# Two decoder layers on one core: order of TensorE work in the attention and delta-rule branches

## The chip, the cores and the metric

The kernel runs on one core of a Trainium2 chip. The metric is the device time of one execution, in microseconds; a kernel's time is the median of its runs. The core has five engines, each with its own instruction queue that is worked through in order: PE (TensorE, matrix products, with its weight loads shown apart as PEld), DVE (VectorE), ACT (ScalarE), POOL (GpSimd) and SP (SyncE, which here only issues DMAs). ACT can issue DMAs too, from the same queue that holds its arithmetic.

## The reference

Two layers, each on 512 tokens of width 1024:

```
xn   = rmsnorm(x)
proj = xn @ w_in                 # columns for all branches and three gate blocks
A    = SSD: causal conv, chunked scan, SiLU-gated rmsnorm
B    = latent attention: q = rmsnorm(cq) @ w_uq  (8 heads, 128 plain + 64 rotated columns each)
       k_nope, v = rmsnorm(ckv) @ w_ukv ; one rotated key shared by the heads ; causal softmax
C    = gated delta rule, chunks of 64:
       (I + a_mat) sol = rhs     # triangular solve in each chunk and head
       v_new = u - w state ; o = q state + qk v_new ; state = state*decay + k^T v_new
h    = x + (sum over branches of sigmoid(gate) * (branch @ w_branch)) @ w_out
x    = h + relu(rmsnorm(h) @ w_up)^2 @ w_down
```

A final rmsnorm follows the second layer. All inputs and outputs are float32.

## The kernel before

**Dense products.** Each float32 operand is split into a high part and a low rest (`hi`, `lo`), and one product is made of three matmuls: hi·hi, hi·lo and lo·hi. The helper `mm3` (lines 178 to 182) issues these three; in this document one call is a *triple*, and its third matmul is line 182. `dense_F` gives a result with features on the partitions, `dense_T` one with tokens there. `weights` (line 162) loads a block of a weight matrix from SP into one of two raw buffers (`wraw`) and splits it with an ACT copy (line 158) and a DVE subtraction (line 159) into one of four pairs `whi`/`wlo`. Results go to four PSUM banks named `acc`; the small products of the branches share three banks named `sm` and one named `yt`.

**Order.** The program is written branch by branch, but a planner that works with estimated costs orders each engine's queue when the program is built: of the instructions whose inputs it takes to be ready, it issues the one written first. The order is then fixed, and what is late on the chip is waited for. An extra dependency without a semaphore (`add_manual_dep` with `NoSync`) tells the planner that one instruction must come after another of the same engine; nothing is waited for at run time because of it.

**Latent attention (head pairs from line 636).** For each of four head pairs: the queries' projection (`q_weights`, 12 triples in three banks: two heads' plain parts and one bank with both rotated parts), the rotation of the queries (`rope`, line 603: four DMAs that swap halves, then three DVE operations; line 676: two more DMAs that swap the heads), the keys' projection (4 triples), the values' projection (8 triples in four banks, line 692), and then for each head scores (lines 703 to 708), softmax, transposes (line 725) and the product with the values (lines 741 to 743). The DMAs of lines 607 and 676 are issued by ACT. Each values' bank is 128x256 and is moved out in two pieces of 128 columns, each with an ACT copy (line 251) and a DVE subtraction (line 252).

**Delta rule.** `gdn_matrix` and `gdn_blocks` build the chunk matrices and invert their 32x32 blocks on DVE; `gdn_inverses` (line 941) joins the blocks into 64x64 inverses with products of 32x32 (lines 956, 966, 968) and 64x64 (lines 977, 981), between which ACT and DVE copy results from PSUM. Meanwhile dense triples of the SSD branch run. `gdn_unit` (line 984) runs twice, for four heads each: after its own projections it walks over four chunks of 128 tokens, and in each come `keys` (line 1036), the solve (line 1042), the state's update (1056), the output's products (1065, 1070). At the end of a unit four groups of transposes (line 1096) turn its result for the output projection.

**Output projections.** `out_proj` goes over four column blocks: first the gate's projection and a tanh, then the branch's projection, which is multiplied with the gate and added to `mixed`.

Order of writing in a layer, counted in triples from the start of attention: attention 0 to 95, keys of the delta rule 96 to 127, SSD group 0 to 207, (inverses), two blocks of attention's output to 271, SSD group 1 to 351, attention's and SSD's outputs to 543, delta-rule unit 0 to 623, unit 1 to 703, delta-rule output 704 to 831. In the first layer 64 triples precede attention (32 each of the two latent projections).

Of the kernel before, what the change touches and what calls it, by code (L numbers as in the profile page):

```python
# [20 lines left out]
P = 128  # L21
S = 512
# [37 lines left out]
def hybrid_kernel(ctx, tc, a, out, depth=2, taps=None):  # L60
# [91 lines left out]

    def split_half(raw, hold=None):

        n = raw.shape[1]
        hi, lo = hold or (mk(wp, [P, n], F32R, "whi"), mk(wp, [P, n], F32R, "wlo"))
        with tc.high_priority():
            act.copy(hi, raw)  # L158
            dve.tensor_tensor(lo, raw, f32(hi), ALU.subtract)  # L159
        return hi, lo  # L160
# [16 lines left out]

    def mm3(o, ah, al, bh, bl, start, stop, more=False):

        pe.matmul(o, ah, bh, start=start, stop=False, skip_group_check=more)  # L180
        pe.matmul(o, ah, bl, start=False, stop=False, skip_group_check=more)  # L181
        pe.matmul(o, al, bh, start=False, stop=stop, skip_group_check=more)  # L182
# [239 lines left out]
    for ly in range(depth):  # L422
# [119 lines left out]
        def seg_exp(pl, o, t, h0):  # L542
# [4 lines left out]
            pe.matmul(ps, w, cum[1][:, t].rearrange("p i l -> p (i l)"), start=True, stop=True)  # L547
# [5 lines left out]

        def out_proj(w2d, br, yh, yl, pl, part=range(4)):
            for dp in part:
                tg = []
                for ps in dense_F(weights(w_in, O_GATE + br * D + dp * 256, 256, D), tiles(256), D, xh, xl):
                    t_ = mk(pl, [P, S], F32, "cva", 2)
                    act.activation(t_, ps, AF.Tanh, scale=0.5)
                    tg.append(t_)  # L560
                for j, ps in enumerate(dense_F(weights(w2d, dp * 256, 256, D), tiles(256), D, yh, yl)):
                    d = 2 * dp + j
                    if mixed[d] is None:
                        mixed[d] = mk(lp, [P, S], F32, "mix", 8)
                        dve.scalar_tensor_tensor(mixed[d], tg[j], 1.0, ps, ALU.add, ALU.mult)
                    else:
                        dve.scalar_tensor_tensor(tg[j], tg[j], 1.0, ps, ALU.add, ALU.mult)
                        dve.tensor_tensor(mixed[d], mixed[d], tg[j], ALU.add)


# [32 lines left out]
        def rope(src):  # L603

            sw_ = mk(lp, [P, S], F32, "mix", 8)
            for i in range(4):
                act.dma_start(sw_[32 * i : 32 * i + 32], src[32 * (i ^ 1) : 32 * (i ^ 1) + 32])
# [26 lines left out]
        scale = (128 + 64) ** -0.5  # L634
        yh, yl = hilo_tags(lp, "y")
        for hp in range(4):
            def q_weights():
                for k0 in (0, 2):
                    raw = mk(wp, [P, 768], F32, "wraw", 2)
                    sync.dma_start(raw.rearrange("p (k n) -> p k n", k=2),  # L640
                                   a["mla_w_uq"][ly][k0 * P : (k0 + 2) * P, hp * 384 : (hp + 1) * 384].rearrange("(k p) n -> p k n", p=P))
                    for k in range(2):
                        rv = raw[:, k * 384 : (k + 1) * 384].rearrange("p (h n) -> p h n", h=2)
                        hi = mk(wp, [P, 384], F32R, "whi")
                        lo = mk(wp, [P, 384], F32R, "wlo")
                        nv = lambda x: x[:, :256].rearrange("p (h n) -> p h n", h=2)
                        pv = lambda x: x[:, 256:].rearrange("p (h n) -> p h n", h=2)
                        act.copy(nv(hi), rv[:, :, :P])
                        act.copy(pv(hi), rv[:, :, P:])
                        dve.tensor_tensor(nv(lo), rv[:, :, :P], f32(nv(hi)), ALU.subtract)  # L650
                        dve.tensor_tensor(pv(lo), rv[:, :, P:], f32(pv(hi)), ALU.subtract)
                        yield k0 + k, hi.unsqueeze(1), lo.unsqueeze(1)

            *pq, pp = dense_F(q_weights(), tiles(384), 512, cqh, cql)

# [13 lines left out]
            qs = head_tiles(pq, "q", scale)  # L669
# [5 lines left out]
            for i in range(2):  # L675
                act.dma_start(qd[64 * i : 64 * i + 64], qr[64 * (1 - i) : 64 * (1 - i) + 64])
            qps = [mk(ml, [P, S], F32R, f"qps{j}") for j in range(2)]
            for j in range(2):
                half, other = (slice(64 * i, 64 * i + 64) for i in (j, 1 - j))
                act.copy(qps[j][half], qr[half])  # L680
                dve.tensor_tensor(qpl[j][half], qr[half], f32(qps[j][half]), ALU.subtract)
                act.copy(qps[j][other], qd[other])
# [5 lines left out]
            def ev(t, ps):  # L688
                for j in range(2):
                    split_act(*(x[:, t, :] for x in vs[j]), ps[:, j * P : (j + 1) * P])  # L690

            dense_T(wkv, 256, 256, ckh, ckl, ev, lambda w: w.rearrange("p (h n) -> p h n", h=2)[:, :, P:])

            for j in range(2):
# [3 lines left out]
                for t in range(T):  # L698
# [4 lines left out]
                    pe.matmul(o, qh[:, tok], kh[:, :n], start=True, stop=False)  # L703
                    pe.matmul(o, qh[:, tok], kl[:, :n], start=False, stop=False)
                    pe.matmul(o, ql[:, tok], kh[:, :n], start=False, stop=False)
                    pe.matmul(o, qps[j][:, tok], kps[:, :n], start=False, stop=False)  # L706
# [13 lines left out]
                for kbs in ((0,), (1,), (3, 2)):  # L720
                    ps = sm_bank()
                    n = 0
                    for kb in kbs:
                        for t in range(kb, T):
                            pe.transpose(ps[:, n : n + P], pn[t][:, kb * P : (kb + 1) * P], ident)  # L725
# [11 lines left out]
                    for kb, c0, c in parts:  # L737
                        v_h, v_l = (x[:, kb, :] for x in vs[j])
                        o = po[:, c0:]
                        w = S - c0  # L740
                        pe.matmul(o, v_h, th[:, c : c + w], start=kb == 0, stop=False)  # L741
# [30 lines left out]
        def ssd_group(g, yh, yl):  # L772
# [14 lines left out]
            for t in range(T):  # L787
                pe.transpose(ps[:, t * P : (t + 1) * P], bt[:, t * P : (t + 1) * P], ident)
            act.activation(btok.rearrange("p t n -> p (t n)"), ps, AF.Copy, scale=0.25)
            for cp in range(2):  # L790
                for j, pj in enumerate(dense_F(weights(w_in, O_XBC + 512 * g + 256 * cp, 256, D), tiles(256), D, xh, xl)):
# [3 lines left out]
                    for t in range(T):  # L795
                        pe.transpose(ps[:, t * P : (t + 1) * P], xf[:, t * P : (t + 1) * P], ident)
# [5 lines left out]
            for t in range(T):  # L802
# [13 lines left out]
                for h in range(8):  # L816
                    pe.matmul(py[:, h * 64 : (h + 1) * 64], e2[h // 4][:, h % 4, :], xd[:, h * 64 : (h + 1) * 64], start=True, stop=True)  # L817
# [28 lines left out]
            for c in range(4):  # L846
                k = 4 * g + c
                ps = y_bank()
                for t in range(T):
                    pe.transpose(ps[:, t * P : (t + 1) * P], z[:, t, c * P : (c + 1) * P], ident)  # L850
# [90 lines left out]
        def gdn_inverses(nts, xs):  # L941
# [9 lines left out]
            for u in range(2):  # L951
                ps = sm_bank()
                q = mk(br, [P, 512], F32, "eE", 2)
                for ev_, od in zip(EV, OD):
                    for i in range(16):
                        pe.matmul(ps[od, i * 32 : (i + 1) * 32], N[u][ev_, i, od], xs[u][ev_, i, :32], start=True, stop=True)
                act.copy(q[OD[0]], ps[OD[0]])
                dve.tensor_copy(q[OD[1]], ps[OD[1]])
                qs.append(q)
            for u in range(2):  # L960
                ps = sm_bank()
                q = qs[u]
                for p_, (ev_, od) in enumerate(zip(EV, OD)):
                    for i in range(16):
                        c = slice(i * 32, (i + 1) * 32)
                        pe.matmul(ps[ev_, c], q[od, c], N[u][od, i, od], start=True, stop=True)
                        if p_ == 0:
                            pe.matmul(ps[od, c], N[u][od, i, od], q[od, c], start=True, stop=True)
                dve.tensor_copy(xs[u][OD[0], :, :32], v32(ps[OD[0]]))
                for ev_, od in zip(EV, OD):  # L970
                    act.copy(N[u][ev_, :, od], v32(ps[ev_]))
            for u in range(2):
                for i0 in (0, 8):
                    ps = sm_bank()
                    q = mk(br, [P, 512], F32, "eE", 2)
                    for i in range(8):
                        pe.matmul(ps[64:, i * 64 : (i + 1) * 64], N[u][:64, i0 + i, 64:], xs[u][:64, i0 + i, :], start=True, stop=True)
                    (dve.tensor_copy if i0 else act.copy)(q[64:], ps[64:])
# [425 lines left out]
```

## Time and profile before

| | |
|---|---|
| runs | 2360.38, 2364.24, 2359.33 us; median 2360.38 |
| the profiled execution | 2360.41 us, its span 2358.6 us |
| PE, share of the span | 99% (PEld 81%) |
| DVE, ACT, POOL | 68%, 48%, 3% |
| mean granted TensorE clock | 0.995 |
| DMA, mean | 94 GB/s |

The span runs from the first to the last instruction; 1.8 us lie around it. A row of groups reads: line, engine, operation, out<-in, shapes, count, then busy time and the mean of one instruction, then the engine's idle time just before them and what ended it. A row of waits reads: who waited, for whom, total, number, longest. A window's row reads: from:to, length, busy time and count of instructions by engine, granted clock, DMA. The durations of matmuls are modelled to the end of their pipeline, so two that follow each other overlap in the profile.

### The profile page before, as it was taken

How to read it: one execution, taken by the hardware profiler on the slowest of the kernel's cores; microseconds unless marked ns; L12 is line 12 of the kernel's file. 1: busy time of each engine (PE TensorE's matmuls, PEld its weight loads, DVE VectorE, ACT ScalarE, POOL GpSimd, SP SyncE). 2: the span in 40 equal slices, each digit the busy share in tenths (PEclk: the TensorE clock that was granted, in tenths of full speed). 3: DMA queues.
4: the chain of work that ended last, by engine and by line, in shares of the span. 5: the costliest groups of instructions: out<-in, count | busy, mean ns of one | idle time of the engine just before them, and what ended most of it. 6: DMA issues, size and time to landing. Idle time of an engine off the chain costs nothing.

```text
span 2358.6 us, 32004 instructions
## 1 busy us (share of the span) xinstructions
PE 2323.6 (99%) x11901; PEld 1911.4 (81%) x11902; DVE 1595.8 (68%) x3183; ACT 1131.9 (48%) x2267; POOL 61.6 (3%) x76
## 2 busy tenths in 40 slices
PE   9999999999999999999999999999999999999998
PEld 7878778888887888888887877888888878888886
DVE  7878865635675468767767789665356655677668
ACT  6655524423343345545656555344234434455545
POOL 1000000000000000000000000000000100000000
PEclk9999999999999999999999999999999999999999
DMA  4222432233222443233132223322333224332231
GB/s 136 85 68 81 117 88 81 81 90 96 84 77 76 137 150 107 71 126 116 40 106 72 72 84 104 97 81 81 98 90 85 76 81 157 129 108 89 90 125 45
DMA packets 196509, 222.77 MB, mean 94 GB/s; under 512 B 31105, under 2 KB 152449, under 8 KB 196353
## 3 DMA queue, kind: packets, MB, share of 16 engines
q1 hardware_dynamic: 193008, 215.92, 30.0%
q10 hardware_dynamic: 3344, 4.80, 0.8%
q8 instruction: 94, 1.54, 0.3%
q14 instruction: 63, 0.51, 0.1%
HBM read 204.44 MB, written 11.53 MB: 92 GB/s over the span
## 4 chain that ended last, share of the span: by engine, by line
PE 92%; DVE 4%; DMA 1%; ACT 1%; POOL 1%; issue 1%; SPq 0%; ACTq 0%; POOLq 0%; DVEq 0%
PE acc L180 23%; PE acc L181 23%; PE acc L182 23%; PE sm L181 2%; PE sm L180 2%; PE sm L182 2%; PE sm L817 1%; PE sm L725 1%; PE sm L1042 1%; PE sm L1065 1%; DVE wlo L159 1%; PE yt L741 1%; DMA mix<-mix 1%; PE sm L1056 1%; PE sm L706 0%
## 5 line engine op out<-in xcount | busy, mean ns | idle before, releaser
L159 DVE TENSOR_TENSOR wlo<-wraw,whi 128x512 fp32r<-128x512 f32 (+1 forms) x552 | 376.8, 685 | 428.0 <-ACT whi L158 421.8
L158 ACT CAST whi<-wraw 128x512 fp32r<-128x512 f32 (+1 forms) x552 | 339.7, 618 | 651.9 <-PE acc L181 456.6
L180 PE MATMUL acc<-xh,whi 128*128 128x512 f32 (+1 forms) x1184 | 458.9, 389 | 2.5 <-DVE vl L252 2.5
L182 PE MATMUL acc<-xh,wlo 128*128 128x512 f32 (+1 forms) x1184 | 459.9, 389 | 0.0
L181 PE MATMUL acc<-xl,whi 128*128 128x512 f32 (+1 forms) x1184 | 458.9, 388 | 0.0
L180 PEld LDWEIGHTS acc<-xh,whi 128*128 128x128 f32 x1184 | 222.9, 189 | 45.7 <-issue 1.8
L182 PEld LDWEIGHTS acc<-xh,wlo 128*128 128x128 f32 x1184 | 223.2, 189 | 43.8 <-issue 0.7
L181 PEld LDWEIGHTS acc<-xl,whi 128*128 128x128 f32 x1184 | 223.3, 189 | 43.5 <-issue 0.5
L182 PE MATMUL acc<-yh,wlo 128*128 128x512 f32 x384 | 151.9, 396 | 0.0
L181 PE MATMUL acc<-yl,whi 128*128 128x512 f32 x384 | 151.2, 394 | 0.0
L180 PE MATMUL acc<-yh,whi 128*128 128x512 f32 x384 | 151.2, 397 | 0.0
L158 ACT CAST whi<-wr 128x512 fp32r<-128x512 f32 x160 | 99.6, 622 | 104.8 <-DVE wlo L159 37.5
L182 PE MATMUL acc<-whi,xl 128*128 128x512 f32 (+1 forms) x352 | 134.3, 384 | 0.0
L180 PE MATMUL acc<-whi,xh 128*128 128x512 f32 (+1 forms) x352 | 134.0, 382 | 0.0
L181 PE MATMUL acc<-wlo,xh 128*128 128x512 f32 (+1 forms) x352 | 133.7, 380 | 0.0
L761 DVE SCALAR_TENSOR_TENSOR cva<-acc,pc,cva 128x511 f32<-128x511 f32 (+2 forms) x168 | 119.7, 743 | 15.0 <-ACT cva L759 8.3
L159 DVE TENSOR_TENSOR wlo<-wr,whi 128x512 fp32r<-128x512 f32 x160 | 109.9, 688 | 28.6 <-ACT whi L158 28.4
L182 PE MATMUL acc<-whi,yl 128*128 128x512 f32 (+1 forms) x260 | 100.4, 386 | 0.0
L180 PE MATMUL acc<-whi,yh 128*128 128x512 f32 (+1 forms) x260 | 100.4, 386 | 0.0
L181 PE MATMUL acc<-wlo,yh 128*128 128x512 f32 (+1 forms) x260 | 100.3, 386 | 0.0
L180 PEld LDWEIGHTS acc<-yh,whi 128*128 128x128 f32 x384 | 71.6, 188 | 16.9 <-ACT yh L255 2.3
L181 PEld LDWEIGHTS acc<-yl,whi 128*128 128x128 f32 x384 | 72.2, 188 | 15.4 <-issue 1.0
(406 smaller groups left out, 4542.5 us busy)
## 6 DMA issues: line engine op xcount, KB each, us to landing
wraw<-in_w_in_dram SPq DMA_DIRECT2D x140, 512.0 KB, 3.7
wraw<-in_w_up_dram SPq DMA_DIRECT2D x64, 512.0 KB, 3.7
wr<-in_w_down_dram SPq DMA_DIRECT2D x32, 1024.0 KB, 5.1
wraw<-in_w_mla_out_dram SPq DMA_DIRECT2D x16, 512.0 KB, 3.5
wraw<-in_w_ssd_out_dram SPq DMA_DIRECT2D x16, 512.0 KB, 3.4
wraw<-in_w_gdn_out_dram SPq DMA_DIRECT2D x16, 512.0 KB, 3.4
wraw<-in_w_out_dram SPq DMA_DIRECT2D x16, 512.0 KB, 3.7
wraw<-in_mla_w_uq_dram SPq DMA_DIRECT2D x16, 384.0 KB, 3.3
```

The costliest lines, as they stand in the source:

```text
L158: act.copy(hi, raw)
L159: dve.tensor_tensor(lo, raw, f32(hi), ALU.subtract)
L180: pe.matmul(o, ah, bh, start=start, stop=False, skip_group_check=more)
L181: pe.matmul(o, ah, bl, start=False, stop=False, skip_group_check=more)
L182: pe.matmul(o, al, bh, start=False, stop=stop, skip_group_check=more)
L725: pe.transpose(ps[:, n : n + P], pn[t][:, kb * P : (kb + 1) * P], ident)
L741: pe.matmul(o, v_h, th[:, c : c + w], start=kb == 0, stop=False)
L761: dve.scalar_tensor_tensor(acc[:, d:], ps[:, : S - d], taps_[3 - d], acc[:, d:], ALU.mult, ALU.add)
L817: pe.matmul(py[:, h * 64 : (h + 1) * 64], e2[h // 4][:, h % 4, :], xd[:, h * 64 : (h + 1) * 64], start=True, stop=True)
L1042: m = pe.matmul(pw[:, h * P : (h + 1) * P], Y[:, h, :], r[:, h * P : (h + 1) * P], start=True, stop=True)
L1056: pe.matmul(pS[:, i * 256 : (i + 1) * 256], ktok[i][:, t, :], vd[:, i * 256 : (i + 1) * 256], start=True, stop=True)
L1065: pe.matmul(po[:, h * P : (h + 1) * P], pt_[:, h, :], vn[:, h * P : (h + 1) * P], start=True, stop=True)
```

## The change

Five edits. (1) The small products and some copies of the delta rule get a key when they are written (`step`), and at the end of a layer `hold_steps` adds a dependency without a semaphore from each one whose key is in the table `BEHIND` to the dense triple of that number (for ACT and DVE: to the last weight split before it). Keys that begin with 0 and a text hold in the first layer only. (2) In attention the queries' rotated part is projected first, in one bank and from weights laid out for it (`uq_r`, `uq_n` are host-side rearrangements of the same matrix), then rotated; the plain parts come after. (3) The values go to two banks of 128x512, each moved out with one copy and one subtraction. (4) The swaps of the rotation go to SP's queue, where the weight loads are. (5) The delta rule's output projection computes the gates of block 0 and 1 before the first branch projection, and stays one block ahead.

```diff
+    BEHIND = {
+        ("solve", 0, 1): 634, ("solve", 0, 3): 669, ("attend", 0, 3): 671, ("solve", 1, 1): 714,
+        ("solve", 1, 2): 723, ("solve", 1, 3): 739, ("out", 0, 0): 687, ("out", 0, 1): 691, ("out", 1, 0): 756,
+        (0, "pair", 1): 311, (0, "left", 0): 314, (0, "right", 0): 317, (0, "left", 1): 319, (0, "right", 1): 322,
+        (0, "paired", 1): 315,
+    }
+    def hold_steps(ly, n):
+        for key, ins in steps:
+            keys = [k[:i] for k in ((ly,) + key, key) for i in range(len(k), 0, -1)]
+            at = next((n + BEHIND[k] for k in keys if k in BEHIND), None)
+            if at is not None:
+                on = triples[at] if ins.engine == pe.engine else next(x[ins.engine] for i, x in reversed(splits) if i <= at)
+                tc.add_manual_dep(ins, on, ... NoSync ...)
...
+        def out_proj_ahead(w2d, br, yh, yl, pl):
+            for dp in (0, 1, None, 2, None, 3, None, None):   # a number: gates; None: the next projection
...
         def rope(src):
-                act.dma_start(sw_[32 * i : 32 * i + 32], src[32 * (i ^ 1) : 32 * (i ^ 1) + 32])
+                sync.dma_start(sw_[32 * i : 32 * i + 32], src[32 * (i ^ 1) : 32 * (i ^ 1) + 32])
...
-            *pq, pp = dense_F(q_weights(), tiles(384), 512, cqh, cql)
-            qs = head_tiles(pq, "q", scale)
+            raw = mk(wp, [P, 512], F32, "wraw", 2)
+            sync.dma_start(raw, a["uq_r"][ly][hp])
+            wh, wl = split_half(raw)
+            pp = acc_bank()
+            for k in range(4):
+                mm3(pp, wh[:, kc], wl[:, kc], cqh[k], cql[k], k == 0, k == 3)
             qp = mk(ml, [P, S], F32, "qp")
             act.mul(qp, pp, scale)
             qr = rope(qp)
-                act.dma_start(qd[64 * i : 64 * i + 64], qr[64 * (1 - i) : 64 * (1 - i) + 64])
+                sync.dma_start(qd[64 * i : 64 * i + 64], qr[64 * (1 - i) : 64 * (1 - i) + 64])
...
+            qs = head_tiles(dense_F(weights(a["uq_n"][ly], hp * 256, 256, 512), tiles(256), 512, cqh, cql), "q", scale)
...
-            vs = [[mk(ml, [P, T, P], F32R, nm, 2) for nm in ("vh", "vl")] for _ in range(2)]
-            dense_T(wkv, 256, 256, ckh, ckl, ev, lambda w: ...)
+            vs = [mk(ml, [P, T, 256], F32R, nm, 1) for nm in ("vh", "vl")]
+            for q in range(2):
+                ps = acc_bank()
+                for t in (2 * q, 2 * q + 1):
+                    o = ps[:, t % 2 * 256 : t % 2 * 256 + 256]
+                    ... mm3(o, ckh[k0 + k][:, tok], ckl[k0 + k][:, tok], vw(wh[:, k, :]), vw(wl[:, k, :]), ...)
+                split_act(*(x[:, 2 * q : 2 * q + 2].rearrange("p t n -> p (t n)") for x in vs), ps)
...
-        out_proj(a["w_gdn_out"][ly], 2, *yg, br)
+        out_proj_ahead(a["w_gdn_out"][ly], 2, *yg, br)
+        hold_steps(ly, n_mla)
```

More of the change, by code (lines that the diff above doesn't have):

```diff
@@ L150, in rope_tables @@
         act.activation(cosT, nn, AF.Sin)
+    triples = []
+    splits = []
     def split_half(raw, hold=None):
@@ L157, in split_half @@
         with tc.high_priority():
-            act.copy(hi, raw)
-            dve.tensor_tensor(lo, raw, f32(hi), ALU.subtract)
+            pair = act.copy(hi, raw), dve.tensor_tensor(lo, raw, f32(hi), ALU.subtract)
+        splits.append((len(triples), {i.ins.engine: i.ins.name for i in pair}))
         return hi, lo
@@ L181, in mm3 @@
         pe.matmul(o, ah, bl, start=False, stop=False, skip_group_check=more)
-        pe.matmul(o, al, bh, start=False, stop=stop, skip_group_check=more)
+        triples.append(pe.matmul(o, al, bh, start=False, stop=stop, skip_group_check=more).ins.name)
     def dense_F(gen, cols, K, xh, xl, mid=None, banks=None):
@@ L552, in hybrid_kernel, with gates, project @@
         mixed = [None] * KD
+        def gates(br, dp, tg):
+            for t_, ps in zip(tg, dense_F(weights(w_in, O_GATE + br * D + dp * 256, 256, D), tiles(256), D, xh, xl)):
+                act.activation(t_, ps, AF.Tanh, scale=0.5)
+            return tg
+        def project(w2d, yh, yl, dp, tg):
+            for j, ps in enumerate(dense_F(weights(w2d, dp * 256, 256, D), tiles(256), D, yh, yl)):
+                d = 2 * dp + j
+                if mixed[d] is None:
+                    mixed[d] = mk(lp, [P, S], F32, "mix", 8)
+                    dve.scalar_tensor_tensor(mixed[d], tg[j], 1.0, ps, ALU.add, ALU.mult)
+                else:
+                    dve.scalar_tensor_tensor(tg[j], tg[j], 1.0, ps, ALU.add, ALU.mult)
+                    dve.tensor_tensor(mixed[d], mixed[d], tg[j], ALU.add)
@@ L554, in out_proj, with pair_tiles @@
+        def pair_tiles(pl):
+            return [mk(pl, [P, S], F32, "cva", 2) for _ in range(2)]
         def out_proj(w2d, br, yh, yl, pl, part=range(4)):
             for dp in part:
[L556 to L568, printed above, removed]
+                project(w2d, yh, yl, dp, gates(br, dp, pair_tiles(pl)))
@@ new lines, in out_proj_ahead @@
+        def out_proj_ahead(w2d, br, yh, yl, pl):
+            tg = {}
+            for dp in (0, 1, None, 2, None, 3, None, None):
+                if dp is None:
+                    d = min(tg)
+                    project(w2d, yh, yl, d, tg.pop(d))
+                    continue
+                if dp % 2:
+                    both = mk(pl, [P, 2, S], F32, "bA" if dp == 1 else "bB")
+                    tg[dp] = gates(br, dp, [both[:, j] for j in range(2)])
+                else:
+                    tg[dp] = gates(br, dp, pair_tiles(pl))
@@ L634, in hybrid_kernel @@
         scale = (128 + 64) ** -0.5
+        n_mla = len(triples)
         yh, yl = hilo_tags(lp, "y")
         for hp in range(4):
[L637 to L652, printed above, removed]
-            *pq, pp = dense_F(q_weights(), tiles(384), 512, cqh, cql)
             def head_tiles(pss, nm, c=None):
@@ L1035, in gdn_unit @@
                     for i in range(2):
-                        pe.matmul(pk[:, i * 256 : (i + 1) * 256], kT[i][:, tok], st[:, i * 256 : (i + 1) * 256], start=True, stop=True)
+                        step(pe.matmul(pk[:, i * 256 : (i + 1) * 256], kT[i][:, tok], st[:, i * 256 : (i + 1) * 256], start=True, stop=True), "keys", u, t)
                     for h in range(4):
@@ L1370, in hybrid_kernel @@
     h_pool.close()
[L1373 removed]
+_INS = ['x', 'positions', 'w_in', 'mla_w_ukv', 'w_ssd_out', 'w_mla_out', 'w_gdn_out', 'w_out', 'w_up',
         'w_down', 'final_norm_g']
```

75 lines of the change are left out of this document (43 added, 32 removed).

## The prediction

> **What bounds the kernel now.** I read the page's busy shares first, then its chain, then the list of who waited for whom on PE, then the granted clock by stretch, and last the queues of ACT and SP in attention.
>
> ```profile
> PE 2323.6 (99%) x11901; PEld 1911.4 (81%) x11902; DVE 1595.8 (68%) x3183; ACT 1131.9 (48%) x2267; POOL 61.6 (3%) x76
> PE 92%; DVE 4%; DMA 1%; ACT 1%; POOL 1%; issue 1%; SPq 0%; ACTq 0%; POOLq 0%; DVEq 0%
> ```
>
> PE sets the time: 99% busy and 92% of the chain. The change takes away no matmul, so it can gain only where PE waits or runs slowly. The waits:
>
> ```profile
> engine line waited for: us in total, times, longest us
> PE acc L180 <- DVE vl L252: 6.2, 5, 1.7
> PE sm L1042 <- DVE tok L1038: 3.1, 6, 0.6
> PE yt L1096 <- DVE tok L1091: 3.0, 4, 0.9
> PE sm L547 <- DVE sg L545: 2.5, 3, 1.2
> ...
> PE sm L706 <- ACT qps L682: 1.3, 2, 0.7
> ...
> PE sm L981 <- DVE eE L978: 0.9, 1, 0.9
> ...
> PE sm L981 <- ACT eE L978: 0.7, 1, 0.7
> PE sm L966 <- ACT eE L957: 0.7, 1, 0.7
> ```
>
> Five lines are what the edits aim at: the values' eviction (vl), the delta rule's solves (L1042) and output transposes (L1096), the rotated part (L706), the inverses (L981, L966). A wait costs a little more than its idle time, because a matmul's shown end lies behind the point at which its successor may start:
>
> ```profile
> 104.23 0.39 PE L182 MATMUL acc<-cqh,wlo 128*128 128x512 f32 x1
> 104.45 0.39 PE L180 MATMUL acc<-cqh,whi 128*128 128x512 f32 x1
> ```
>
> Each lasts 0.39 us and the next starts after 0.23 (a triple is 0.68 us), so I add 0.16 us a wait. (The Trainium skill, "Trainium Kernel Development and Optimization", Performance Expectations, says that matmul busy time is a bad metric because matmuls are pipelined; the 0.39 against 0.23 agrees.) The clock:
>
> ```profile
> 330.42:387.57 57.15, 54.87 (x592) 0.88 0.26 71
> 1506.58:1556.80 50.22, 50.16 (x594) 1.00 0.27 72
> 351.12:364.78 13.66, 12.71 (x102) 10.73 (x101) 3.87 (x6) 5.07 (x9) 0.00 (x0) 0.50 0.26 79
> 1245.41:1248.83 3.42, 3.36 (x8) 2.71 (x9) 2.89 (x9) 0.93 (x5) 0.00 (x0) 0.50 0.59 183
> ```
>
> The first two rows (PE alone) are the same work, the delta rule's inverses with SSD triples around them, in the first and the second layer: 592 and 594 matmuls, 57.15 and 50.22 us. The first layer loses 6.9 us, to the three waits of L966 and L981 and to a stretch of 13.7 us at half clock; the second has neither. The last row is half clock for 3.4 us just behind the second layer's longest vl wait.
>
> **The change part by part.**
>
> *Values in two banks.* Before, four banks are finished together at the end of the values' product and leave in eight pieces:
>
> ```profile
> L251 ACT CAST vh<-acc 128x128 fp32r<-128x128 f32 x64 | 14.3, 277 | 4.7 <-PE acc L182 2.6 <-DVE vl L252 1.5 <-issue 0.2
> L252 DVE TENSOR_TENSOR vl<-acc,vh 128x128 fp32r<-128x128 f32 x64 | 15.2, 282 | 0.0
> L158 ACT CAST whi<-wraw 128x512 fp32r<-128x512 f32 x536 | 332.3, 622 | 640.0 <-PE acc L181 456.6 <-PE acc L182 88.6 <-PE yt L181 25.3
> L159 DVE TENSOR_TENSOR wlo<-wraw,whi 128x512 fp32r<-128x512 f32 x536 | 368.7, 690 | 415.4 <-ACT whi L158 409.3 <-ACT cva L757 1.8 <-PE acc L182 1.5
> ```
>
> Eight pieces are 8 x 0.28 = 2.2 us on each of ACT and DVE; two pieces of 512 columns, by the same operations on 512 columns (L158, L159), 1.2 and 1.4. The first bank now ends half way through the product, and the next dense product needs one bank (the rotated part) where it needed three, while two of four were never taken by values. I let all five waits go: 6.2 + 5 x 0.16 = **7.0 us**, and with them the 3.4 us at half clock, half of it, **1.7 us**. Cover: the keys' two banks must be out before the values end; if not, one eviction, 0.62 + 0.69 = 1.3 us, is paid at each of eight head pairs.
>
> *Rotated part first, swaps on SP.* The order of ACT's queue before one of the vl waits (its end at 130.88):
>
> ```profile
> 126.61 0.55 ACT L251 CAST vh<-acc 128x128 fp32r<-128x128 f32 x2
> 126.90 0.55 ACTq L607 DMA_DIRECT2D mix<-qp  x1
> 127.05 0.41 ACT L648 CAST whi<-wraw 128x256 fp32r<-128x256 f32 x1
> 127.48 1.25 ACTq L607 DMA_DIRECT2D mix<-qp  x2
> 129.22 0.59 ACT L251 CAST yh<-yt 128x512 fp32r<-128x512 f32 x1 [1.76 <-PE yt L743]
> 129.23 0.51 ACTq L607 DMA_DIRECT2D mix<-qp  x1
> 129.78 0.77 ACT L251 CAST vh<-acc 128x128 fp32r<-128x128 f32 x4
> 74.69 0.37 SPq L171 DMA_DIRECT2D wraw<-in_mla_w_ukv_dram  x1
> ```
>
> Four DMA issues stand between the second and the third vh copy, about 0.55 us each. With the two of L676 a head pair spends 6 x 0.55 = 3.3 us of ACT on issues; on SP one takes 0.37 (last row), 2.2 us, and SP has nothing else to do but load. The rotation, which needs two DMAs in a row, now starts 8 triples (5.5 us) earlier against its scores. L706's two waits go: 1.3 + 2 x 0.16 = **1.6 us**. The queries' weights also become three splits of 512 columns in place of eight smaller ones. None of this ACT and DVE time is on the chain by itself; I give it no term.
>
> What SP's move could cost: SP is in order, and its loads wait long.
>
> ```profile
> SPq L171 <- DVE wlo L651: 36.0, 3, 15.4
> 133.01 4.50 DMA mix<-mix
> 1279.04 4.29 DMA mix<-mix
> wraw<-in_mla_w_ukv_dram SPq DMA_DIRECT2D x8, 512.0 KB, 3.6
> ```
>
> A load waits up to 15.4 us for its raw buffer, and a swap queued behind it would wait as well; a load behind a swap waits for the rotation. Loads have time to spare (3.6 us to land against waits of 9 to 15 us for a place), so I take 0; the upper end is one slow swap (4.5 us, the longest rows of the chain) on the path at each of eight head pairs, 36 us, which is the slower rival below. The Trainium skill, "DMA: Bandwidth & Descriptors", Issuing engines are not separate DMA queues, says that issuing from several engines saves only the sequencer's time; by it the move is free, while the same page, Queues, rings and completion order, has each issuing engine own a ring that is drained in order, so that a swap would stand behind a 512 KB load: 3.6 us more for each of two steps. No row here shows swaps on SP's ring.
>
> *Held products.* The numbers in the table against where the products stand now (windows of line 182 alone, the third matmul of a triple; 64 precede the count in the first layer):
>
> ```profile
> 0.00:626.15 626.15, 268.59 (x697) 131.34 (x697) 0.99 0.32 92
> 0.00:661.50 661.50, 282.71 (x732) 137.91 (x732) 0.99 0.32 91
> 0.00:706.00 706.00, 300.90 (x777) 146.30 (x777) 0.99 0.31 90
> 0.00:729.50 729.50, 308.02 (x794) 149.56 (x794) 0.99 0.31 89
> 0.00:737.50 737.50, 310.45 (x800) 150.68 (x800) 0.99 0.31 89
> 0.00:347.25 347.25, 135.30 (x360) 67.63 (x360) 1.00 0.34 98
> ```
>
> The solves that wait stand behind 633, 668 and 713 triples and are held behind 635, 670 and 715 (a number n in the table means n + 1 issued): two triples, 1.36 us, against waits of 0.6 at most and their 0.16. All six go: 3.1 + 6 x 0.16 = **4.1 us**. The chain of chunks behind them moves by the same 1.4 us; the planner moves what follows with it. The output transposes of unit 1 wait at 717 and 737; they are now held behind the triple 756 of 832, where the later one stood behind 736, and the gates computed ahead are the dense work that fills the distance: 3.0 + 4 x 0.16 = **3.6 us**. If the cover were short, they would wait as now. In the last solve's place there is a longer delay (730 to 740 triples, 6.8 us); what waits for it are the transposes alone, 17 triples further on, against 8.0 us from solve to transpose now (729.5 to 737.5). The inverses of the first layer: `pair` stands behind 296 triples with no triple up to 357 us, and is held behind 312, then 2 to 5 triples between each step. If that makes the first layer like the second: **6.9 us**.
>
> *Sum.* 7.0 + 1.7 + 1.6 + 4.1 + 3.6 + 6.9 = 24.9 us. Against it stands that the queue orders are planned anew and that the planner's errors, which made these waits, stay. Lower bound of new waits: none. Upper: every head pair and every held place waits again as long as now, (6.2 + 1.3)/7 + 0.16 = 1.2 us at eight head pairs and 7.7 us in the delta rule, 17.3 us. I take 5, nearer to none, since each removed wait had a cause of its own that is gone. 24.9 - 5 = 19.9. The profiled execution took 2360.41 us, as the median (2360.38): **2340.5 us**.
>
> **The rivals.**
>
> A: the holds only move the waits (the solve's chain through DVE is what is late, and two triples less of cover are missing one chunk on). For it: six waits of almost equal size, one in three chunks. Against: other chunks don't wait. Attention alone: 7.0 + 1.7 + 1.6 = 10.3, time **2350**.
>
> B: the first layer's clock doesn't come back. For it: half clock began at 351.1 behind waits of 0.7 us, so the small products themselves may be too little activity. Against: the second layer runs them at full clock. Of the 6.9 us the waits are 0.9 + 0.7 + 0.7 + 3 x 0.16 = 2.8; 4.1 stay, and perhaps the 1.7: **2345**. The Trainium skill, "TensorE: Matmul & The Clock Gate", HAM oscillation, puts re-throttling to idle gaps over about 3.4 us; by it waits of 0.7 us would not matter. The rows disagree, as no gap here is that long and the clock fell.
>
> C: slower. SP's order puts a swap behind a load that waits for its raw buffer. Place: L706 of each head pair; price: what the swap is late beyond the cover. It decides from 24.9 / 8 = 3.1 us a head pair; at 4.5 us the sum is -24.9 + 36 = +11: **2371**. For it the 15.4 us row; against it that qp is now ready early, and that a raw buffer is freed by splits that PE's own pace sets.
>
> D: no change: new waits (17.3 and more) eat the gain; within 0.2% of before, **2358**.
>
> **How the numbers follow.** Forecast 0.55, A 0.12, B 0.14, C 0.10, D 0.09. About 0.2% (4.7 us) is what this kernel's runs can tell. A, B and the forecast are faster: 0.81, less 0.01 for A's edge; same 0.09; slower 0.10. Range: below, all 24.9 us and the L547 waits (2.5 + 0.5) by a lucky order, 2332; I go to 2330. Above, 24.9 - 17.3 = 7.6 gives 2353, and D's edge takes it to 2357. Forecast's own range 2333 to 2349.
>
> **What would show it.** Right: no row of PE waiting for vl, at most one for L1038 and L1091, the first layer's stretch of inverses at clock 1.00 and about 50 us, no half clock in attention, L607 and L676 on SP. Wrong: rows of L706 waiting for qps or a DMA (C), L1042 still waiting (A), a stretch at 0.50 near the held inverses (B). The whole is wrong if PE's waits shrink and the span doesn't.

## The result

The changed kernel takes **2335.47 us** (median of 4 runs, 2334.5 to 2340.46) against 2361.04 for the kernel before (4 runs beside it, 2359.33 to 2364.24): ratio 0.9896, 95% interval 0.9881 to 0.9911. That is 25.6 us less. The forecast was 2340.5, its range 2330 to 2357. The profiled execution took 2336.03 us (span 2334.1, mean clock 0.998).

The busy shares and the shares of the chain, from the changed kernel's page:

```profile
PE 2314.3 (99%) x11902; PEld 1908.0 (82%) x11902; DVE 1590.1 (68%) x3095; ACT 1123.9 (48%) x2179; POOL 60.1 (3%) x76
PE 95%; DVE 2%; ACT 1%; DMA 1%; POOL 0%; issue 0%; SPq 0%; POOLq 0%; ACTq 0%; DVEq 0%
```

PE's part of the chain went from 92% to 95%, DVE's from 4% to 2%; PE still sets the time. Who waited for whom on PE, in the changed kernel:

```profile
PE sm L574 <- DVE sg L572: 3.7, 4, 1.2
...
PE acc L207 <- ACT cqh L282: 1.2, 2, 0.6
...
PE sm L856 <- DVE eE L851: 0.5, 1, 0.5
...
PE sm L745 <- ACT qps L716: 0.3, 1, 0.3
```

The values' wait (vl, 6.2 us), those for `tok` of the solves (3.1) and output transposes (3.0) and the three in the inverses are gone. The decays of SSD (L574, which was L547) wait longer than before: 3.7 us in 4 against 2.5 in 3. New are 1.2 us for `cqh`, once in each layer at the first products of the queries, and 0.5 us for `eE` at a scan product.

To see where the time went, both executions are cut at the same counts of triples, and PE alone is shown in each stretch. Triples are counted here from the start of the program; layer 2's numbers are 1457 higher. Only triples are counted, so a small product can lie on another side of a cut in another kernel. In order: attention of layer 1 (triples 64 to 160), what follows it (to 224, then to 347), the inverses of layer 1 (to 400), delta-rule units 0 and 1 of layer 1 (680 to 770, to 860), the start of the output projection (890 to 960), attention and inverses of layer 2 (1521 to 1617, 1804 to 1857). Before:

```profile
51.71:158.81 107.10, 104.00 (x601) 1.00 0.25 72
158.81:221.42 62.61, 61.12 (x310) 1.00 0.27 74
221.42:329.88 108.46, 107.11 (x511) 1.00 0.40 113
329.88:394.80 64.92, 62.63 (x628) 0.89 0.26 72
609.08:697.10 88.02, 87.03 (x456) 1.00 0.27 78
697.10:779.82 82.72, 80.58 (x391) 1.00 0.27 77
800.22:850.95 50.73, 49.69 (x228) 1.00 0.44 146
1227.20:1336.62 109.42, 105.25 (x590) 0.98 0.26 75
1506.03:1564.01 57.98, 57.92 (x628) 1.00 0.28 73
```

After, the same nine stretches:

```profile
51.65:153.47 101.82, 100.71 (x580) 1.00 0.26 73
153.47:216.86 63.39, 63.37 (x325) 1.00 0.28 75
216.86:327.86 111.00, 108.32 (x515) 1.00 0.35 103
327.86:385.18 57.32, 57.28 (x628) 1.00 0.37 93
599.50:685.99 86.49, 86.49 (x455) 1.00 0.29 80
685.99:766.00 80.01, 80.01 (x391) 1.00 0.27 80
786.40:836.38 49.98, 49.66 (x227) 1.00 0.45 148
1213.10:1315.50 102.40, 102.26 (x590) 1.00 0.25 73
1484.83:1544.13 59.30, 59.24 (x628) 0.97 0.28 72
```

The counts of matmuls (x) show that the first three stretches of layer 1 do not hold the same work: after the change there are 21 fewer in the first, 15 and 4 more in the next two. So the 5.3 us of the first stretch can't be read alone. The three together hold the same matmuls, and go from 278.17 to 276.21 us, 2.0 less. By PE's idle time (length less busy time) 2.0 + 1.5 = 3.5 us are gained in attention and just behind it, and 1.3 us are lost in the third stretch, where the decays (sg) and the scan product (eE) wait.

The other gains: attention of layer 2 7.0 us with the same work, the inverses of layer 1 7.6 (their clock went from 0.89 to 1.00), each unit pair 1.5 + 2.7 = 4.2 (the second layer's pair gives the same), the output projection's start 0.75. The inverses of layer 2 are 1.3 us longer, because of a stretch at half clock; the order of PE's instructions there is the same in both kernels, so the loss can't be put down to the new order:

```profile
1511.76:1515.17 3.41, 3.41 (x17) 0.50 0.08 10
```

### The profile page after: what moved, and what is told of

Read it like the earlier page. It is cut to its first block, busy times and chain, and to the rows that moved or that the text cites. A ratio compares the mean times of both kernels' runs of the same rounds, so it can differ in the third digit from the quotient of the medians.

```text
span 2334.1 us, 31810 instructions
## 1 busy us (share of the span) xinstructions
PE 2314.3 (99%) x11902; PEld 1908.0 (82%) x11902; DVE 1590.1 (68%) x3095; ACT 1123.9 (48%) x2179; POOL 60.1 (3%) x76
## 4 chain that ended last, share of the span: by engine, by line
PE 95%; DVE 2%; ACT 1%; DMA 1%; POOL 0%; issue 0%; SPq 0%; POOLq 0%; ACTq 0%; DVEq 0%
PE acc L207 24%; PE acc L208 24%; PE acc L209 24%; PE sm L208 2%; PE sm L209 2%; PE sm L207 2%; PE sm L856 1%; PE sm L764 1%; PE yt L780 1%; PE sm L1104 1%; PE sm L1081 1%; PE sm L1095 1%; PE sm L742 0%; PE sm L745 0%; PE sm L862 0%; PE yt L208 0%
## 5 line engine op out<-in xcount | busy, mean ns | idle before, releaser
L161 DVE TENSOR_TENSOR wlo<-wraw,whi 128x512 fp32r<-128x512 f32 (+1 forms) x576 | 392.4, 684 | 427.4 <-ACT whi L161 421.2
L161 ACT CAST whi<-wraw 128x512 fp32r<-128x512 f32 (+1 forms) x576 | 353.9, 618 | 664.9 <-PE acc L208 462.3
L209 PEld LDWEIGHTS acc<-yh,wlo 128*128 128x128 f32 x384 | 72.3, 188 | 15.1 <-issue 0.7
```

The source lines that it names most:

```text
L161: pair = act.copy(hi, raw), dve.tensor_tensor(lo, raw, f32(hi), ALU.subtract)
L209: triples.append(pe.matmul(o, al, bh, start=False, stop=stop, skip_group_check=more).ins.name)
```

## The experiments

All stretches below are cut at the same counts of triples. "Waits" are rows of PE's waits of the kernel in question; lines are shifted by a few from kernel to kernel.

**All holds away (e1).** The changed kernel with the three attention edits only.

```diff
-    BEHIND = { ... }
+    BEHIND = {}
-        out_proj_ahead(a["w_gdn_out"][ly], 2, *yg, br)
+        out_proj(a["w_gdn_out"][ly], 2, *yg, br)
```

> The changed kernel with an empty table of holds and the gates not ahead: the attention edits alone. Theory (the edits act apart, by stage): attention keeps its 12 us against the kernel before, the delta-rule units lose their 8.5 us again with waits of L1081 and L1135 (solve and output transposes) of about 6 us, and the first layer's inverses lose 5 to 8 us: 2349 to 2353 us. Rival (attention's gain needs nothing else and the holds only undo what the new attention order does to the plan): near 2361. Rival (the holds are superfluous once the plan has changed): 2335 to 2338.

Measured 2349.72 us (2348.04 to 2352.07), ratio 0.9958 (0.9944 to 0.9972), in the range of its theory. Its waits:

```profile
PE sm L1076 <- DVE tok L1072: 3.1, 6, 0.6
PE yt L1130 <- DVE tok L1125: 3.0, 4, 0.9
...
PE sm L1015 <- DVE eE L1012: 0.9, 1, 0.9
```

The delta rule's waits are back to the digit. The inverses of layer 1 take 62.89 us, and their clock is low again (0.92), with one wait of 0.9 us for eE. The three attention edits together are worth 10.7 us (against 2360.39 of the kernel before beside it; 2.0 of it lie in layer 1's inverses, 64.92 to 62.89), the holds and the gates 14.3 (against 2335.47).

**The inverses' holds away (e2).** The six entries from `pair` to `paired` are left out.

> The changed kernel without the six holds of the first layer's inverses. Theory: waits of the small products and a stretch at half clock come back in the first layer's inverses, that stretch takes 63 to 66 us instead of 57.3, all else unchanged: 2341 to 2344 us. Rival (the new plan keeps the inverses covered in any case): same time, 2335.

Measured 2342.5 us (2339.95 to 2344.82), ratio 0.9927 (0.9912 to 0.9942). Its inverses of layer 1 and of layer 2:

```profile
327.21:390.08 62.87, 61.25 (x628) 0.92 0.33 85
1489.43:1547.45 58.02, 57.96 (x629) 1.00 0.29 75
```

The first stretch is 62.87 us at clock 0.92 in place of 57.32 at 1.00: the holds alone give 5.5 us. Attention's edits had taken 64.92 to 62.9 by themselves. The time is the theory's, the stretch 0.1 us below its range. "All else unchanged" was not so in the profiled execution: layer 2's inverses, whose order is the changed kernel's, took 58.02 us in place of 59.30.

**The units' holds away (e7), and the gates not ahead (e6).** e7 drops the nine entries of the delta rule's units and keeps the gates ahead; e6 keeps the holds and puts the gates back, with one number altered:

```diff
-        ("solve", 0, 1): 634, ... ("out", 0, 1): 691, ("out", 1, 0): 756,       # e7: all nine away
-        ... ("out", 1, 0): 756,                                               # e6
+        ... ("out", 1, 0): 746,
-        out_proj_ahead(a["w_gdn_out"][ly], 2, *yg, br)
+        out_proj(a["w_gdn_out"][ly], 2, *yg, br)
```

> Changed: the changed kernel without the nine holds of the delta rule's units (solves, one attend, output transposes); the gates ahead and the six inverse holds stay. Theory: it is these holds that took the waits away. The solves wait for tok again (3.1 us in 6) and the transposes for their results (3.0 in 4 at most); units' stretches back to about 88.0 and 82.7 us, 4.2 more in each two of two layers, 8.5 in all; time 2341 to 2344. Rival (the gates computed ahead give the planner enough dense work, and the holds add nothing to unit 1): unit 1's stretches stay near 80.0, only unit 0's go back, 3 us; time 2337 to 2340.

> Changed: the delta rule's output projection computes each block's gates just ahead of its branch projection again, as in the kernel before; all holds stay, but unit 1's transposes are held behind triple 746, not 756, because the projection that needs them now begins earlier. Theory (the holds make the gain, the gates ahead only fill the distance): the waits of the solves stay away in both units, unit 0's stretch (triples 680 to 770) stays at 86.4 us, unit 1's (770 to 860) at 80.0 to 81.5; time 2335 to 2338. Rival (the transposes are late without the gates as filler): the two waits of unit 1's transposes for tok come back, 1.5 us with what a wait costs, and dense work runs out behind them, unit 1's stretch 82 to 84 and the start of the output projection (890 to 960) 0.7 longer; time 2338 to 2341.

e7 took 2343.11 us (2342.54 to 2345.84), ratio 0.9926 (0.9911 to 0.9941). Units 0 and 1 of layer 1, and two of its waits:

```profile
602.30:690.34 88.04, 87.05 (x455) 1.00 0.27 78
690.34:772.78 82.44, 80.22 (x391) 1.00 0.27 77
```

```profile
PE yt L1133 <- DVE tok L1128: 3.2, 4, 1.0
PE sm L1079 <- DVE tok L1075: 3.1, 6, 0.6
```

e6 took 2340.43 us (2337.35 to 2343.01), ratio 0.9912 (0.9895 to 0.9928). Unit 1 of layer 1, and its wait:

```profile
686.46:768.13 81.67, 80.49 (x392) 1.00 0.27 78
```

```profile
PE yt L1135 <- DVE tok L1130: 1.9, 2, 1.0
```

With the gates ahead but no holds, unit 1 gains 0.3 us (82.72 to 82.44); with holds but without the gates, 1.05 (to 81.67); with both, 2.7. In unit 0 the holds do it alone. So e7's theory holds; in e6 the stretch lies between the two expectations and the time is the rival's: one transpose per layer has nothing dense left to stand behind. The cover that the prediction named for the transposes, the gates, is real, and its price without it is 1.7 us a layer in unit 1.

**Each attention edit taken out of the changed kernel (e3, e4, e5).**

```diff
-                sync.dma_start(sw_[32 * i : 32 * i + 32], ...)               # e3, and the swap of heads
+                act.dma_start(sw_[32 * i : 32 * i + 32], ...)
-            vs = [mk(ml, [P, T, 256], F32R, nm, 1) for nm in ("vh", "vl")]    # e4: as in the kernel before
+            vs = [[mk(ml, [P, T, P], F32R, nm, 2) for nm in ("vh", "vl")] for _ in range(2)]
             raw = mk(wp, [P, 512], F32, "wraw", 2)                            # e5: plain parts written first
+            qs = head_tiles(dense_F(weights(a["uq_n"][ly], ...)...), "q", scale)     # moved ahead of these lines
```

> The changed kernel with the swaps of the rotation issued by ACT again. Theory (the values' four banks were what made PE wait, ACT's DMA issues only lengthened it): attention longer by 0 to 2 us, 2335 to 2338 us, no waits for vl. Rival (the DMA issues in ACT's queue were the cause): waits for vl or qps return, 5 to 8 us, 2340 to 2344.

> The changed kernel with the values in four banks and eight pieces as before, all other edits kept. Theory: waits for vl return in both layers, 4 to 7 us: 2339 to 2343 us. Rival (ACT's free queue and the rotated part first are enough): no waits for vl, 2335 to 2337.

> The changed kernel with the queries' plain parts projected before the rotated part, all else kept. Theory (what the runs with swaps on ACT and with four banks showed: a head pair paces the plan, and any delay of the rotation or of the evictions pushes the last heads behind the dense work that covers them): the rotation starts 8 triples (5.5 us) later in each head pair, the head pair's period grows from 29 to over 30 us, and half or more of attention's gain goes: 2341 to 2355 us. Rival (the order in a head pair does not matter once the swaps are on SP): 2335 to 2338 us.

| kernel | time, us | ratio to before, interval |
|---|---|---|
| e3, swaps on ACT | 2361.17 | 1.0002 (0.9993 to 1.0012) |
| e4, four banks | 2359.69 | 0.9999 (0.999 to 1.0008) |
| e5, plain parts first | 2352.99 | 0.9961 (0.9946 to 0.9976) |

e5 lies in the range of its theory; e3 and e4 miss both expectations by 16 us and more: taking away **either** edit takes with it as much as the whole change gives, delta rule included. In e3 the first layer's attention (64 to 160) and what follows (to 224), then the third matmuls of value products (PE, then PEld) in the 11.2 us from 187.70 on:

```profile
51.51:150.17 98.66, 94.42 (x534) 1.00 0.26 75
150.17:227.38 77.21, 72.80 (x375) 1.00 0.23 62
187.70:198.90 11.20, 2.19 (x7) 1.14 (x7) 1.00 0.16 47
```

The triples of the first stretch are issued *faster* than in the changed kernel (98.66 us against 101.82), with 46 fewer small products between them; those come later, and 77.21 us pass where the changed kernel takes 63.39. The changed kernel's last value product ends by 187.7; e3 has seven left, until 198.9, and only two dense triples run beside them. The delay is seen in the DMA issues of the third head pair (time, duration of one or all, queue), with the product of the second pair's first head and the values (L781) ahead of it. The changed kernel, and what SP waited for there:

```profile
116.59 0.40 PE L781 MATMUL yt<-mix,vh 128*128 128x512 f32 x1
117.02 2.45 SPq L653 DMA_DIRECT2D mix<-qp  x4
SPq L653 <- PE yt L781: 4.9, 1, 4.9
```

and e3:

```profile
123.81 0.50 PE L781 MATMUL yt<-mix,vh 128*128 128x512 f32 x1
132.65 0.55 ACTq L653 DMA_DIRECT2D mix<-qp  x1
```

The swap of the third pair is 15.6 us later on ACT. On SP it goes 0.4 us behind L781, for which SP had waited (the swap writes one of the eight `mix` buffers, and L781 reads one). In e3 L781 itself comes 7.2 us later, and the swap's first issue another 8.8 us behind it, between copies of the second head, which are written earlier and so go first on ACT. So about half of the delay is the place in ACT's queue, and the rest is that everything ahead is late already. (The Trainium skill, "DMA: Bandwidth & Descriptors", Issuing engines are not separate DMA queues, says that initiating DMAs on several engines at once saves only the sequencer's time. The issues themselves agree, some 0.6 us on both; what differs is how long an issue stands in an in-order queue behind other work.) The heads' small products finish late, and the dense triples beside them have been used up.

Of the 24.0 us between the two spans, 10.7 and 7.2 lie in triples 64 to 224 of layer 1 and the same of layer 2, and 6.7 and 3.3 in the inverses (64.02 and 62.64 us, with half clock in both), though the six holds are in place; the stretches between gain 2.7 and 1.0. Of e3's waits here, those of the first row (2.5 and 2.6 us) come at the ends of the two attentions, where a dense product waits for the convolution to free a bank; the 3.6 us of the second row are in the inverses of layer 1:

```profile
PE acc L207 <- DVE cva L800: 5.2, 2, 2.6
PE acc L207 <- ACT whi L161: 3.8, 2, 3.6
```

e4 loses at the values instead, as the kernel before did, only more: 10.2 us in its waits, and a first attention of 115.78 us (which begins at 54.87 where the changed kernel's begins at 51.65: ahead of it, at 12.18, is a stretch of 3.41 us at half clock; e7, which has the changed kernel's attention, has one at 11.76 and begins at 54.40):

```profile
PE acc L207 <- DVE vl L279: 10.2, 5, 4.0
```

```profile
54.87:170.65 115.78, 107.96 (x605) 0.96 0.22 64
```

e5 has e3's pattern: 94.13 us, then 76.16. The period of a head pair, which its theory had grow from 29 to over 30 us, grew little (between the swaps of heads of the first and the fourth pair of layer 1, 29.7 to 30.2 us on average).

```profile
52.18:146.31 94.13, 93.17 (x537) 1.00 0.28 82
146.31:222.47 76.16, 71.86 (x374) 1.00 0.23 63
```

**Each of two attention edits alone, on the kernel before (b1, b2).**

```diff
-            vs = [[mk(ml, [P, T, P], F32R, nm, 2) ...] ...]      # b1: only the values in two banks
+            vs = [mk(ml, [P, T, 256], F32R, nm, 1) ...]
-                act.dma_start(sw_[32 * i : 32 * i + 32], ...)   # b2: only the swaps on SP
+                sync.dma_start(sw_[32 * i : 32 * i + 32], ...)
```

> The kernel before with the values in two banks as its only edit. Theory of the prediction (each edit removes its own waits): the waits for vl go, 6 to 9 us: 2352 to 2355 us. Rival (attention's edits only pay together, since the plan is made anew from the slowest chain): 2357 us or more.

> The kernel before with the swaps of the rotation on SP as its only edit. Theory of the prediction: the vh copies are no longer held up by DMA issues in ACT's queue and L706's waits go: 2 to 6 us, 2355 to 2359 us. Rival (only together): 2359 us or more, with the vl waits unchanged. Rival C of the prediction (swaps behind loads): L706 waits for a DMA or for qps and the time is over 2365 us.

b1 took 2373.23 us (2370.76 to 2374.56), ratio 1.0048 (1.0033 to 1.0063): **slower by 11.6 us**. No wait for vl is left, but:

```profile
PE sm L710 <- ACT qps L682: 10.2, 5, 3.2
```

The banks that come free let the planner issue dense triples earlier (triples 64 to 160 of layer 1 take 103.51 us in place of 107.10, with 58 fewer small products between them), and the rotation, still last and still on ACT, is then late: 10.2 us in five waits in place of 1.3 in two, and 73.79 us up to triple 224 in place of 62.61. b2 took 2359.64 us (2358.97 to 2362.55), ratio 0.9992 (0.9983 to 1.0002). Its attention is faster (3.9 us from triple 64 to 224, 5.9 in layer 2 over the same triples), and the rows for vl and qps are both gone, with the values still in four banks; 2.9 us are lost behind attention in layer 1 (to triple 347), where the decays wait, and the largest part in the inverses of layer 2:

```profile
1499.04:1564.76 65.72, 63.93 (x628) 0.87 0.28 71
```

That is 65.72 us where the kernel before takes 57.98. The edit touches nothing but attention, and yet the order of PE's instructions at the inverses, over 100 us later, is another one.

**Better numbers (e8, e9, e10).** Three attempts to take what was left. e8 lets the inverses' six holds act in both layers. e9 adds holds for what still waits; e10 adds to e9 six holds for layer 2 with numbers of its own. In e9's expectation "five more holds in the first layer" is a slip: two of the five stand in the second, as the diff shows and e10's text says.

```diff
-        (0, "pair", 1): 311, (0, "left", 0): 314, ...           # e8: keys without the layer
+        ("pair", 1): 311, ("left", 0): 314, ...
+        (0, "decay", 16, 1): 186, (0, "decay", 20, 3): 201, (1, "decay", 16, 2): 176, (1, "decay", 20, 2): 195,   # e9, e10
+        (0, "scan", 0, 0): 219,
+        (1, "pair", 1): 303, (1, "left", 0): 305, (1, "paired", 1): 306, (1, "right", 0): 308, (1, "left", 1): 310, (1, "right", 1): 313,   # e10
```

> The changed kernel with the six holds of the inverses in both layers. Theory (long stretches of small products with few dense triples between, not waits, let the clock fall, in some executions and not in others): the second layer's stretch of inverses goes from 58.0 to 59.3 us to about 57.3, never a half clock there, 1 to 2 us faster: 2333.5 to 2335 us, and the runs lie closer together. Rival (waits are what lets the clock fall; there is none here): no change, 2335 to 2336 us.

> Changed: the changed kernel with five more holds in the first layer: the two late pairs of the SSD decays' small products (written 16 and 20 groups in, that is the four waits for sg, 3.7 us in all) stand some triples later, and the first scan product (0.5 us wait) too. Theory (every wait behind an estimate that was too early goes the same way as the solves'): the row of waits for sg and the one for eE at the scan go, 4.2 + 5 x 0.16 = 5.0 us less at most, and about 1 us stays since later products move too; the stretch from triple 160 to 347 goes from 174.4 to about 171; time 2331 to 2334. Rival (DVE is what is late there, and the wait only moves to its next product): a new wait of PE for DVE in the same stretch, no less in all; time 2335 to 2338.

> Changed: the kernel with the five holds of the decays and the scan (three of them in the first layer, two in the second), and beside them six holds for the second layer's inverses with numbers of its own: pair where it stands anyway (triple 303), then two or three triples between each step up to 313, as the first layer has them. What the kernel without these six showed: the first layer's stretches 2 us shorter, the second layer's 160 to 347 stretch 1.4 shorter, and its inverses 64.1 us in place of 59.3, behind a new wait of 0.7 us for eE and one for whi. Theory (spread between dense triples that have their weights, the second layer's small products keep the clock as the first layer's do): that stretch (triples 1804 to 1857) 57.5 to 59.5 us, no wait for eE there; time 2330 to 2333. Rival (the weight splits, behind the convolution on ACT and DVE, run out again as soon as triples are pulled ahead): a wait of a triple for whi or wlo of over 1 us and half clock behind it, stretch 62 to 66; time 2335 to 2339.

| kernel | time, us | ratio to before, interval |
|---|---|---|
| e8 | 2341.62 (2340.97 to 2342.4) | 0.9917 (0.99 to 0.9933) |
| e9 | 2337.12 (2334.89 to 2341.78) | 0.9901 (0.9886 to 0.9916) |
| e10 | 2338.07 (2335.61 to 2338.44) | 0.9899 (0.9882 to 0.9915) |

None beats the change: e9 and e10 can't be told from it, e8 is some 6 us slower, outside both its expectations. The holds on the decays work where they stand. e9, layer 1 from triple 224 to 347, and then the inverses of layer 2:

```profile
217.73:326.62 108.89, 107.90 (x514) 1.00 0.37 107
1482.56:1546.67 64.11, 63.22 (x628) 0.89 0.27 69
```

The first is 108.89 us against 111.00 (and no row for sg is left), the second 64.11 against 59.30: more than both layers gain at the decays (2.1 and 1.4) is lost in layer 2's inverses. So e9's theory held for the waits and its rival's range for the time, though not for the rival's reason. e8 and e10 fail in that same stretch, by a wait for whi of 3.6 us in e8 and this one in e10:

```profile
PE acc L209 <- ACT whi L161: 3.7, 1, 3.7
```

```profile
1507.35 0.63 ACT L292 ACTIVATE ft<-cva 128x512 f32<-128x512 f32 x1 [1.48 <-DVE cva L802]
1507.88 1.64 ACT L161 CAST whi<-wraw 128x512 fp32r<-128x512 f32 x3
```

When the small products are held, dense triples are pulled in front of them, and in layer 2 the split of their weights stands on ACT behind the convolution, which itself waits for DVE (second fence, e10). PE is idle for 3.6 to 3.7 us and then runs the next product at half clock. e10's own numbers spread the later steps, but the first triple behind `pair` already lacks its weights, and its stretch takes 65.5 us: the rival of its expectation.

## Why the prediction was right, and where it was not

**The whole.** 19.9 us were predicted and 24.9 came against the median that stood there (2360.38). By the stretches, each compared over the same work:

| term | predicted | measured |
|---|---|---|
| attention (7.0 + 1.7 + 1.6) | 10.3 | 3.5 + 7.0 = 10.5 |
| inverses of layer 1 | 6.9 | 7.6 |
| solves and output transposes (4.1 + 3.6) | 7.7 | 2 x (1.53 + 2.71) = 8.5 |
| start of the output projection, both layers | none | 1.1 (0.75 + 0.36) |
| losses | 5 | 1.3 + 1.3 + 0.5 = 3.1 |

The gains sum to 27.7, and 27.7 - 3.1 = 24.6 is near the difference of the spans (24.5). The losses are the decays in layer 1, the half clock in layer 2's inverses and 0.5 us between the output projection and layer 2 (376.25 to 376.72 us). So the gross sum was 2.8 too small, and the 5 was 1.9 too large. The prediction's bound of 17.3 was built from head pairs and held places, and none of the losses lies there: that 5 came near is luck. In the delta rule the price of a wait held (idle time plus 0.16 us): the holds give 8.5 - 2 x 0.3 = 7.9 for 7.7. What was missing is the gates' own 0.3 a layer (e7) and the start of the output projection, which had no term.

**The inverses.** The argument was that the first layer would come to look like the second. It did: 57.32 at clock 1.00 beside 57.98 before. e2 shows that the holds do it, 5.5 us of it, and that attention's edits gave the other 2. So of the 6.9 us that the prediction gave to the holds, 5.5 are theirs. Layer 2, which the prediction took as the model at full clock, ran 1.3 us longer than before, with one stretch at half clock.

**The holds of the units.** Right by both tests: no row of waiting solves is left, and without the holds (e7) the waits come back at 3.1 us in 6. Rival A (the holds only move the waits) has fallen. That the gates are the cover of the transposes is shown by e6.

**Attention, the step that failed.** The total was near (10.3 for 10.5), but its account was wrong. The prediction priced the values' banks at 7.0 + 1.7 us by themselves, the rotation at 1.6, and SP's relief of ACT at nothing ("None of this ACT and DVE time is on the chain by itself; I give it no term"). The runs: two banks alone remove the waits for vl and still cost 11.6 us (b1). Swaps on SP alone remove the same waits with four banks still in place, and take 3.9 and 5.9 us off the two attentions, but lose it again further on, so that the time does not change measurably (b2). Taken out of the changed kernel the banks are worth 24.2, the swaps 25.7 and the order of the queries 17.5 us. Each figure includes what a new plan does to the rest of the layer (10.0 us in the inverses for the swaps). The edits aren't terms that can be added: with banks free, dense triples go ahead, and then the rotation must be early enough, which takes both its place in the text and a queue in which the copies of the pair before do not stand ahead of it. That all these edits were made together, without which the total would not have come, was no part of the argument, and so luck. The rule that a freed wait is worth its idle time is only good if the order stays, and for a single edit here it does not.

**Rival C.** A swap on SP does hold SP up. The swap of heads in the changed kernel (durations in ns: least, median, most):

```profile
L710 SPq DMA_DIRECT2D mix<-mix x16: 496/553/862, 74.4 to 1318.6; - x16
L710 SPq EVENT_SEMAPHORE  x8: 2015/2581/4609, 72.3 to 1314.9; - x8
```

At each of the eight head pairs SP stands for 2.0 to 4.6 us until the rotation is done, but the loads behind it had that time to spare, as was argued: PE waits for no weight split, and 0.3 us of waiting for qps is left. One detail was wrong: a swap was to take 0.37 us on SP, the duration of a load; it takes 0.55, as on ACT. What SP gives is an earlier place (some 8 of the 15.6 us in the pair shown), not a quicker issue. Nor were 3.3 us of ACT at stake: in the prediction's rows two of the four issues run beside copies (the copy from 127.05 starts within the issue from 126.90), and the copy of yh ahead of the third vh copy waits 1.76 us for PE.

**Rival B.** The clock of layer 1 came back and B fell; but what was said for it, that half clock can begin behind waits of no more than 0.7 us among small products, is borne out by e1: there it begins at 360.33 us, and the only gap on PE in the 10 us before is 0.67 us.

## What to carry to other kernels

When a planner fixes the order of in-order queues, a change that frees a buffer or a queue is a change of the whole order behind it: try its parts alone and left out before pricing them one by one, since one that loses alone can be what the others need. A hold pays where a product is late by a fixed small amount and dense work stands ready behind it; its number belongs to one plan, and the next stretch that must supply the dense work is the place to look for the cost. For a DMA that other work waits for, choose the issuing queue by what stands in it ahead, not by the time of the issue.

## What the runs showed of the hardware

Every stretch at half clock in these profiles, apart from the end of the program, lasted 3.41 us or a multiple of it (13.66 and 3.42 before, 3.41 after). In the kernel before and in e1 those of the first layer's inverses came with gaps of under 1 us on PE among 32x32 and 64x64 products. The Trainium skill, "TensorE: Matmul & The Clock Gate", HAM oscillation, names idle gaps of over about 3.4 us as the cause; the gaps here (0.67 us before the clock falls, 0.95 at the longest) disagree. A section of the same page, A second HAM failure mode: psum-queue depth-cycling, has frequent short idling do it too, and for these two kernels that agrees. For layer 2's stretch in the changed kernel it does not: PE is idle for only 0.06 us of the 12 us before it, which hold small products and nine triples.

```profile
1499.76:1511.76 12.00, 11.94 (x194) 1.00 0.01 1
```

Six kernels have the same order of PE's instructions in layer 2's inverses. Three took 57.98 (before), 58.02 (e2) and 57.94 us (e7), at clock 1.00; three took 59.30 (changed), 59.32 (e1) and 59.27 us (e6), each with one stretch of 3.41 us at half clock. So that one stretch makes the difference of 1.3 us. Why it falls in three of the six was not shown; these are single executions, and a difference of that size in this section says nothing about an edit.
